# A convolution layer in a two-layer encoder trunk: order of its tiles, turning of rows, dealing of taps, and a last layer by split weights

## The chip, the core and the metric

The kernel runs on one core of a Trainium2 chip. A core has five engines that matter here, each with an instruction queue of its own that is worked off in order: TensorE (PE, matrix products; its weight loads are shown apart as PEld), VectorE (DVE), ScalarE (ACT), GpSimd (POOL), and SyncE (SP), which issues most DMAs. The metric is device time of one launch in microseconds (us), lower is better.

## The reference

Two layers in the manner of a Conformer on 256 rows of 1024 channels, all in float32. Each layer is half a SwiGLU feed-forward net (FFN, width 2816), a mixer, and half an FFN again; the first mixer is a convolution module, the second is latent attention. The change is in and around the convolution module:

```
def conv_module(h, w_pw1, w_dw, g_norm, w_pw2):
    u = h @ w_pw1
    a, b = jnp.split(u, 2, axis=-1)
    u = a * jax.nn.sigmoid(b)
    u = lax.conv_general_dilated(u, w_dw[:, None, :], ..., padding=[(30, 0)],
                                 feature_group_count=D_MODEL)
    u = jax.nn.silu(rmsnorm(u, g_norm))
    return u @ w_pw2
```

So: a norm, a product to 2048 columns, a gate, a causal depthwise convolution with 31 taps for each channel, a second norm over the channels, silu, and a last product of 1024 by 1024.

## The kernel before

**Rows and tiles.** The 256 rows are two row blocks of 128 (tb = 0, 1). A tile k or i of the convolution is 128 channels, eight in all, with channels on the partitions and rows along them.

**Weights.** `blocks` lists every weight block of 128x2048 in the order of use; `load_to` issues loads on SP into one of 3 `raw` buffers, then converts each in two pieces to a rounded high part (L160, ACT) and the remainder (L161, DVE) in `hi` and `lo`, of which there are W_BUFS = 4 each. `weights` takes the next block and loads W_BUFS - 2 = 2 ahead. Blocks marked "whole" stay float32 in `raw`. A product by split weights is three TensorE instructions (high by low, high by high, low by high: L242, L245, L246 in `mm3`); a product of plain float32 is one instruction that the trace records twice.

**Order.** The program is written as one sequence; a scheduler places instructions on the engines' queues by a simulated timeline. `urgent` marks what it is to prefer, `order(ins, first)` puts one instruction behind another, and `behind` keeps conversions behind the last urgent instructions of their engine.

**Into the convolution.** The FFN ends in `Rows.finish`: four output tiles (row block, column half) in turn, each added to h (L506); after each, `Plain.early` works on the norm of the convolution's input: squares (L269), a power on POOL (L279), and a matrix with the row factors on its diagonal (L405). `Plain.turn` multiplies h by this matrix on TensorE (L411), which scales and transposes in one plain float32 product, and copies the result with the channel gain to X on ACT and DVE (L420, L422). The second row block is turned in `late`, behind the first tile's products.

**The convolution** (`conv_in`). `products` (L636) makes gate and u of a tile, tiles 0 and 1 by row block, the rest at full width; `glu` (L643, L644) writes V. The taps of eight tiles are dealt to three engines by CONV_DVE (`taps_dve`, L678 to L681), CONV_POOL (`taps_pool`: products with the tap on ACT, L696 and L700, sums on POOL, L701 and L702) and CONV_PE (`taps_pe`, L711: products with a diagonal matrix made earlier at L1113). Tiles 6 and 7 are shared and done by row block. Squares (L723) of each tile are summed over the channels on TensorE (`total`, L729); `ends` adds the shares of tiles 6 and 7 (L802) and sums them last; `normed` makes the row factor (L746, L748, L754), spreads it over the partitions by a product with ones (L756), and writes Z = silu(Y x factor x gain) (L761, L763), for features 0 to 3 also as high and low part (L765, L766).

**Last layer.** Features 4 to 7 first, as plain float32 (L831), then 0 to 3 by split weights; 2 row blocks x 2 column halves, 512 columns each; then the addition to h (L839). The next FFN's rows are turned (L285, L299, L303) between features of the second row block.

Of the kernel before, what the change touches and what calls it, by code (L numbers as in the profile page):

```python
# [19 lines left out]
P = 128  # L20
D = 1024
S = 256
# [17 lines left out]
W_BUFS = 4  # L40
# [6 lines left out]
CONV_DVE = ((0, 0, 31), (2, 0, 31), (4, 0, 31), (5, 0, 31), (7, 0, 13))  # L47
CONV_POOL = ((1, 0, 31), (3, 0, 31), (6, 0, 19))
CONV_PE = ((6, 19, 31), (7, 13, 31))
CONV_FIRST = (0, 1)  # L50
CONV_LAST = (6, 7)

CONV_ORDER = (0, 2, 1, 4, 3, 5, 6, 7)

CONV_PLAIN = 4
# [23 lines left out]
def trunk(ctx: ExitStack, tc: tile.TileContext, x, xt, pos, invf, gains, gfin, wdw,  # L79
# [28 lines left out]
    for i in range(2):  # L108
        for w13, w2 in ((f1w13, f1w2), (f2w13, f2w2)):

            for cc_ in range(5):
                for m in range(2):
                    blocks += [w13[i, m, 2 * cc_ + a_] for a_ in range(2)]
            blocks += [w13[i, a_, 10] for a_ in range(2)]
            blocks += [w2[i, a_] for a_ in range(NF // 2)]
            if w13 is f1w13:
                if i == 0:


                    for m in (-1, -2, 0, 1, 2, 3, 4, 5, 6, 7, -3, -4):  # L120
                        w = cw2[-m - 1] if m < 0 else cw1[m]
                        blocks += [w if -2 <= m < 0 else ("whole", w)]
                        conv_block[m] = len(blocks) - 1
                else:
                    blocks += [wa[0], wa[1], wa[2][:, :1280], wa[3][:, :1280]]
                    blocks += [wuq[2], wuq[0], wukv[0], wukv[1], wuq[1]]
                    blocks += [wo[a_] for a_ in range(H // 2)]
# [13 lines left out]

    def load(src, pieces=1):
        if isinstance(src, tuple):
            raw = rawp.tile([P, HB], F32, tag="raw", name=uid("raw"))
            nc.sync.dma_start(raw, src[1])
            return raw
        n = src.shape[-1]
        raw = rawp.tile([P, HB], F32, tag="raw", name=uid("raw"))
        hi = wp.tile([P, HB], F32R, tag="hi", name=uid("hi"))
        lo = wp.tile([P, HB], F32R, tag="lo", name=uid("lo"))  # L150
        if len(loaded) < 7:

            for i in range(pieces if len(loaded) < 4 else 1):
                c = slice(i * n // pieces, (i + 1) * n // pieces) if len(loaded) < 4 else slice(n)
                fetch(raw[:, c], src[:, c])
        else:
            nc.sync.dma_start(raw[:, :n], src)
        for i in range(pieces):
            c = slice(i * n // pieces, (i + 1) * n // pieces)
            behind(nc.scalar.copy(hi[:, c], raw[:, c]))  # L160
            behind(nc.vector.tensor_sub(lo[:, c], raw[:, c], hi[:, c].bitcast(F32)))  # L161
        return hi, lo
# [36 lines left out]
    xk = const.tile([P, KT, S], F32, name="xk")  # L199
# [66 lines left out]
    def squares(ss, src, n, i, scale_in=1.0, after=()):  # L266
# [4 lines left out]
        for a in after:  # L271
            order(sq, a.ins)

# [110 lines left out]
    class Plain:  # L384

        def __init__(self, gname, act):
# [4 lines left out]
            self.dg = [xp.tile([P, P], F32, tag=f"dR{tb}", name=uid("dR")) for tb in range(NT)]  # L393

        @urgent
        def half(self, tb, i):
            squares(self.ss[tb], h[tb], D, i)
            if tb == 0 and i == 1:

# [3 lines left out]
        def diagonal(self, tb):  # L403
            r = power(self.ss[tb], D, "R")
            nc.vector.tensor_scalar(self.dg[tb], ident, r, None, op0=ALU.mult)  # L405

        @urgent
        def turn(self, tb, q, after=()):
            b = bank("B", "tp")
            for j in range(4):  # L410
                mm = nc.tensor.matmul(b[:, j * P:(j + 1) * P], h[tb][:, (4 * q + j) * P:(4 * q + j + 1) * P],  # L411
                                      self.dg[tb], start=True, stop=True)
                for a in after:
                    order(mm, a.ins)
                self.turned.append(mm)
            for j in range(4):
                k = 4 * q + j
                g = G[:, self.col + k:self.col + k + 1]
                if j % 2 == 0:
# [4 lines left out]
        def early(self, i):  # L424
            self.half(i // 2, i % 2)
            if i % 2 == 1:
                self.diagonal(i // 2)
# [113 lines left out]
    def ffn_in(act, X, make_next, beside):  # L541
        Gh = act.tile([P, NF, S], F32R, tag="Gh", name=uid("Gh"))
        Gl = act.tile([P, NF, S], F32R, tag="Gl", name=uid("Gl"))
        def turn(c, tb, w, g):
# [9 lines left out]
            b = act.tile([P, 512], F32, tag="gb", name=uid("gb"), bufs=3)  # L554
# [7 lines left out]
        for c in range(6):  # L562
# [5 lines left out]
            for m in range(1 if both else 2):  # L568
                parts = weights(KT // kn, X.whole or c > 0 or m > 0)
# [10 lines left out]
                for i, (k, tb, *kinds) in enumerate(steps):  # L580
# [9 lines left out]
                    if X.whole and c == 0 and m == 0:  # L590
                        if i == 5:
                            load_to(4)
# [10 lines left out]
            for tb in range(NT):  # L603
                s = tmp.tile([P, 512], F32, tag="s", name=uid("s"))
                nc.scalar.activation(s[:, :w], u[0, tb][:, :w], AF.Silu, scale=X.r[tb])  # L605
                g = tmp.tile([P, 512], F32, tag="g", name=uid("g"))
                nc.vector.tensor_mul(g[:, :w], s[:, :w], u[0, tb][:, w:] if both else u[1, tb])  # L607
                turn(c, tb, w, g)
# [11 lines left out]
    def conv_in(act, X, make_next):  # L620
# [10 lines left out]
        def products(i, part, t, u):  # L631

            w = loaded[conv_block[i]]
            for k in range(KT):
                c = slice(k * 2 * P + part * P, k * 2 * P + (part + 1) * P)
                mm = nc.tensor.matmul(u[:, t], w[:, c], X.x[:, k, t], start=(k == 0), stop=(k == KT - 1))  # L636
            return mm
# [9 lines left out]

        steps = [(i, tbs(tb)) for tb in range(NT) for i in CONV_FIRST]
        steps += [(i, every) for i in range(KT) if i not in CONV_FIRST]
        for n, (i, t) in enumerate(steps):  # L650
            load_to(conv_block[min(i + 2, KT - 1)] + 1)
            gate, u = bank("A", "gate"), bank("A", "u")
            products(i, 1, t, gate)
            mm = products(i, 0, t, u)
            glu(i, t, gate, u)
            if n == 0:
                X.late((mm,))

        behind(nc.scalar.activation(small.tile([P, 1], F32, tag="silu", name="silu2"), neghalf, AF.Silu))
        load_to(conv_block[-4] + 1)  # L660
        n_used[0] = max(conv_block.values()) + 1
# [7 lines left out]
        def taps_dve(k, j0, j1, t):  # L669
# [4 lines left out]
            for j in range(j0, j1):  # L674
# [4 lines left out]
                else:  # L679
                    nc.vector.scalar_tensor_tensor(out if j == j1 - 1 else y, v, w, y, op0=ALU.mult, op1=ALU.add)  # L680
            nc.vector.tensor_add(out, acc[(j1 - j0) % 2][:, c], out)  # L681

        sums_pool = []

        def taps_pool(k, j0, j1, t):
# [6 lines left out]
            for j in range(j0, j1):  # L692
# [4 lines left out]
                else:  # L697
                    p = act.tile([P, S], F32, tag="prod", name=uid("prod"), bufs=6)
                    p = p[:, :t.stop - t.start]
                    nc.scalar.activation(p, v, AF.Copy, scale=w)  # L700
                    sums_pool.append(nc.gpsimd.tensor_tensor(o, o, p, op=ALU.add))  # L701
            sums_pool.append(nc.gpsimd.tensor_tensor(y[0], y[0], y[1], op=ALU.add))  # L702
# [17 lines left out]
        def square(k, t):  # L720
            if k not in sq:
                sq[k] = act.tile([P, S], F32, tag="sq", name=uid("sq"), bufs=4)
            nc.scalar.activation(sq[k][:, t], Y[:, k, t], AF.Square)  # L723
# [8 lines left out]
        Z = act.tile([P, KT, S], F32, tag="Z", name="Z")  # L732
        Zh = act.tile([P, KT - CONV_PLAIN, S], F32R, tag="Zh", name="Zh")
        Zl = act.tile([P, KT - CONV_PLAIN, S], F32R, tag="Zl", name="Zl")

        rows_order = [*range(KT - CONV_PLAIN, KT), *range(KT - CONV_PLAIN)]
# [3 lines left out]
        zs = []  # L740

        @urgent
        def normed(tb, after=()):

            ms = small.tile([P, 1], F32, tag="msc", name=uid("msc"))
            nc.scalar.activation(ms, msb[tb][:, :1], AF.Identity, scale=1.0 / D, bias=eps)  # L746
            rc = small.tile([P, 1], F32, tag="rc", name=uid("rc"))
            power = nc.gpsimd.tensor_tensor(rc, ms, neghalf, op=ALU.pow)  # L748
            if tb == 0:

                for ins in sums_pool[-4:]:
                    order(ins, power.ins)
            dg = act.tile([P, P], F32, tag="dg", name=uid("dg"), bufs=2)
            nc.scalar.activation(dg, ident, AF.Copy, scale=rc)  # L754
# [4 lines left out]
            for k in rows_order:  # L759
                z = act.tile([P, P], F32, tag="z", name=uid("z"), bufs=6)  # L760
                zs.append(nc.vector.tensor_mul(z, Y[:, k, tbs(tb)], rb[:, :P]))  # L761
                g = G[:, g0 + k:g0 + k + 1]
                nc.scalar.activation(Z[:, k, tbs(tb)], z, AF.Silu, scale=g)  # L763
                if k < KT - CONV_PLAIN:
                    nc.scalar.activation(Zh[:, k, tbs(tb)], z, AF.Silu, scale=g)  # L765
                    nc.vector.tensor_sub(Zl[:, k, tbs(tb)], Z[:, k, tbs(tb)], Zh[:, k, tbs(tb)].bitcast(F32))  # L766
# [28 lines left out]
        def ends(tb, after, after_row):  # L795
# [4 lines left out]
            def add():  # L800
                for k in CONV_LAST:
# [4 lines left out]
                    square(k, t)  # L806
# [9 lines left out]
        ends(0, done[1][n // 2 + 1], done[1][n * 3 // 4 + 1])  # L816
        order(done[1][-3], brow[0].ins)
# [4 lines left out]
        def mm(n, tb, d):  # L822
            f = rows_order[n]
            after = ()
            if (tb, d) == (0, 0):
                after = {4: [sums[1]], 5: [brow[1]]}[n] if n in (4, 5) else ()
            w = loaded[conv_block[-1 - f // 2]]
            c = slice(f % 2 * D + d * 512, f % 2 * D + d * 512 + 512)
            start, stop = n == 0, n == KT - 1
            if f >= KT - CONV_PLAIN:  # L830
                return nc.tensor.matmul(o[tb, d], Z[:, f, tbs(tb)], w[:, c], start=start, stop=stop)  # L831
            else:
                hi, lo = w
                return mm3(o[tb, d], Zh[:, f, tbs(tb)], Zl[:, f, tbs(tb)], hi[:, c], lo[:, c], start, stop, after)

        @urgent
        def add(tb, d):
            c = slice(d * 512, d * 512 + 512)
            nc.vector.tensor_add(h[tb][:, c], o[tb, d], h[tb][:, c])  # L839

        nxt = None
        load_ahead()
        for tb in range(NT):
            for d in range(2):
                o[tb, d] = bank("A", "o")
            for f in range(KT):
                now = [mm(f, tb, d) for d in range(2)]
                if tb == 0 and f == 0:
                    first = now
                if tb == 0 and f == 2:  # L850

                    ends(1, first[1], now[1])
                if tb == 1 and f in (1, 3):
                    nxt.part(0, f // 2)
                if tb == 1 and f == 3:
# [53 lines left out]
    def rope(dst, src, n, cc, sn, tb):  # L909
# [3 lines left out]
        t2 = tmp.tile([P, 512], F32, tag="g", name=uid("rp2"))  # L913
# [14 lines left out]
    def mla_in(act, X, make_next, cc, sn):  # L928
# [36 lines left out]
        def key_rope(u, tb):  # L965
# [3 lines left out]
            for i in range(2):  # L969
                rope(kd[:, i, :], kx.rearrange("p (n i f) -> p n i f", n=1, i=2), 1, cc, sn, tb)  # L970
# [38 lines left out]
        for tb in range(NT):  # L1009
# [8 lines left out]
            rope(q, u.rearrange("p (n i f) -> p n i f", i=2, f=32), H, cc, sn, tb)  # L1018
# [206 lines left out]
```

## Time and profile before

| | us |
|---|---|
| median of three runs (lowest to highest) | 934.76 (934.67 to 935.11) |
| the profiled execution | 934.88 |
| its span, first to last instruction | 932.8 |
| first gate product of the convolution (L636) | 187.6 |
| last start of a tap on TensorE (L711) | 261.8 |
| last layer of the convolution on TensorE | 262.2 to 289.7 |
| DVE waits for POOL's part (L802 behind L702), in all | 1.7 |
| POOL waits for the first product (L701 behind L700) | 8.0 |
| POOL waits for a product at 242.4 | 1.8 |

All times of the form "at 262.2" are us from the span's start. "128*128 128x512" is a product of a 128x128 weight with 512 columns. The durations of TensorE's instructions overlap, so what one costs is the time from its start to the next one's.

### The profile page before, as it was taken

To read this page: it belongs to the slowest core of one execution; us is meant where nothing else is said; L and a number is where in the kernel's file an instruction comes from. 1 tells how busy PE (TensorE), PEld (TensorE's weight loads), DVE (VectorE), ACT (ScalarE), POOL (GpSimd) and SP (SyncE) were. 2 spreads that over 40 slices of the span, in tenths; PEclk is the share of its full clock that TensorE was granted. 3 is DMA by queue.
4 is the path that set the end of the run, shared out by engine and by line. 5 is a ranking of instruction groups with operands and counts; after the bars stand their busy time and mean duration, and the time that the engine had idled before them with its cause. 6 is when DMAs were issued, how large, how long until landed. Compare 5 with 4: busy or idle time off the path is not lost.

```text
span 932.8 us, 12069 instructions
## 1 busy us (share of the span) xinstructions
PE 924.0 (99%) x4394; PEld 771.8 (83%) x4394; DVE 577.0 (62%) x907; ACT 496.0 (53%) x849; POOL 85.2 (9%) x210
## 2 busy tenths in 40 slices
PE   9999999999999999999999999999999999999997
PEld 7888888898967888888888888888898888888886
DVE  5776664489965655655466666644666676656643
ACT  7964443468866444434465445434676574445431
POOL 1000000059920000000000000000200000000000
PEclk9999999999999999999999999999999999999999
DMA  9886775524315876766537677754451467767721
GB/s 338 301 313 234 249 253 193 180 92 141 131 52 209 281 229 225 265 208 231 208 142 274 226 240 251 253 187 142 172 189 46 182 231 246 244 226 254 242 91 45
DMA packets 60826, 191.54 MB, mean 205 GB/s; under 512 B 11232, under 2 KB 33376, under 8 KB 41440
## 3 DMA queue, kind: packets, MB, share of 16 engines
q1 hardware_dynamic: 60192, 190.09, 58.5%
q8 instruction: 34, 0.56, 0.2%
q10 hardware_dynamic: 576, 0.69, 0.2%
q14 instruction: 24, 0.20, 0.1%
HBM read 178.17 MB, written 12.58 MB: 205 GB/s over the span
## 4 chain that ended last, share of the span: by engine, by line
PE 94%; DVE 2%; ACT 2%; DMA 1%; issue 0%; POOL 0%; POOLq 0%; ACTq 0%; DVEq 0%
PE u L242 17%; PE u L245 17%; PE u L246 17%; PE o L245 10%; PE o L242 10%; PE o L246 10%; PE gate L636 3%; PE u L636 3%; PE y L711 1%; DVE lo L161 1%; PE u L251 1%; PE tp L285 1%; PE o L831 1%; DMA raw<-in_f2w 1%; PE sc L1049 0%
## 5 line engine op out<-in xcount | busy, mean ns | idle before, releaser
L161 DVE TENSOR_TENSOR lo<-raw,hi 128x1024 fp32r<-128x1024 f32 (+1 forms) x290 | 339.5, 1212 | 200.3 <-ACT hi L160 200.0
L160 ACT CAST hi<-raw 128x1024 fp32r<-128x1024 f32 (+1 forms) x290 | 288.8, 1049 | 267.1 <-PE u L246 128.1
L242 PE MATMUL u<-lo,Xh 128*128 128x512 f32 x688 | 268.1, 390 | 0.0
L245 PE MATMUL u<-hi,Xh 128*128 128x512 f32 x688 | 267.8, 389 | 0.0
L246 PE MATMUL u<-hi,Xl 128*128 128x512 f32 x688 | 267.7, 390 | 0.0
L242 PEld LDWEIGHTS u<-lo,Xh 128*128 128x128 f32 x688 | 129.2, 188 | 27.2 <-DVE lo L161 0.4
L246 PEld LDWEIGHTS u<-hi,Xl 128*128 128x128 f32 x688 | 129.2, 188 | 26.8
L245 PEld LDWEIGHTS u<-hi,Xh 128*128 128x128 f32 x688 | 129.2, 188 | 26.7
L245 PE MATMUL o<-hi,Gh 128*128 128x512 f32 (+1 forms) x356 | 137.9, 387 | 0.0
L246 PE MATMUL o<-hi,Gl 128*128 128x512 f32 (+1 forms) x356 | 137.7, 387 | 0.0
L242 PE MATMUL o<-lo,Gh 128*128 128x512 f32 (+1 forms) x356 | 137.4, 388 | 0.0
L242 PEld LDWEIGHTS o<-lo,Gh 128*128 128x128 f32 x356 | 66.9, 188 | 13.6
L246 PEld LDWEIGHTS o<-hi,Gl 128*128 128x128 f32 x356 | 66.9, 188 | 13.5
L245 PEld LDWEIGHTS o<-hi,Gh 128*128 128x128 f32 x356 | 66.9, 188 | 13.3
L276 POOL TENSOR_TENSOR ms<-ss 128x1 f32<-128x1 f32 x16 | 4.6, 287 | 635.3 <-ACT junk L269 635.3
L560 DVE TENSOR_TENSOR Gl<-gb,Gh 128x512 fp32r<-128x512 f32 (+1 forms) x48 | 30.9, 644 | 43.6 <-ACT Gh L559 43.6
L559 ACT CAST Gh<-gb 128x512 fp32r<-128x512 f32 (+1 forms) x48 | 28.0, 584 | 53.9 <-DMA gb<-gd 53.7
L680 DVE SCALAR_TENSOR_TENSOR acc<-V,dw,acc 128x256 f32<-128x256 f32 (+1 forms) x160 | 53.9, 416 | 0.0
L700 ACT ACTIVATE prod<-V,dw 128x128 f32<-128x128 f32 (+1 forms) x121 | 46.1, 420 | 3.0 <-POOL odd L701 1.3
L607 DVE TENSOR_TENSOR g<-s,u 128x512 f32<-128x512 f32 (+1 forms) x48 | 30.7, 639 | 12.4 <-PE u L246 12.4
L605 ACT ACTIVATE s<-u,R 128x512 f32<-128x512 f32 (+1 forms) x48 | 31.2, 650 | 6.7 <-ACT Gh L559 3.2
L549 DVE STREAM_TRANSPOSE gt<-g 128x512 f32<-128x512 f32 (+1 forms) x48 | 32.0, 667 | 1.6
(207 smaller groups left out, 838.0 us busy)
## 6 DMA issues: line engine op xcount, KB each, us to landing
raw<-in_f2w SPq DMA_DIRECT2D x66, 1024.0 KB, 4.9
raw<-in_f1w SPq DMA_DIRECT2D x62, 1024.0 KB, 5.0
raw<-in_cw SPq DMA_DIRECT2D x12, 1024.0 KB, 4.7
gd<-gt SPq DMA_DIRECT2D x160, 64.0 KB, 3.2
gb<-gd SPq DMA_DIRECT2D x40, 256.0 KB, 4.5
raw<-in_wo SPq DMA_DIRECT2D x4, 1024.0 KB, 5.0
raw<-in_wuq SPq DMA_DIRECT2D x3, 1024.0 KB, 4.9
raw<-in_f1w SPq DMA_DIRECT2D x8, 256.0 KB, 5.1
```

The lines of the kernel that those rows point to most:

```text
L160: behind(nc.scalar.copy(hi[:, c], raw[:, c]))
L161: behind(nc.vector.tensor_sub(lo[:, c], raw[:, c], hi[:, c].bitcast(F32)))
L242: mm = nc.tensor.matmul(o, ah, bl, start=start, stop=False)
L245: nc.tensor.matmul(o, ah, bh, start=False, stop=False)
L246: return nc.tensor.matmul(o, al, bh, start=False, stop=stop)
L549: nc.vector.transpose(t[:, :w], g[:, :w].rearrange("p (t j q) -> p j t q", t=n, q=32))
L560: nc.vector.tensor_sub(Gl[:, f, tbs(tb)].rearrange("p t (i q) -> p t i q", q=32), bv, gh.bitcast(F32))
L605: nc.scalar.activation(s[:, :w], u[0, tb][:, :w], AF.Silu, scale=X.r[tb])
L607: nc.vector.tensor_mul(g[:, :w], s[:, :w], u[0, tb][:, w:] if both else u[1, tb])
L636: mm = nc.tensor.matmul(u[:, t], w[:, c], X.x[:, k, t], start=(k == 0), stop=(k == KT - 1))
L680: nc.vector.scalar_tensor_tensor(out if j == j1 - 1 else y, v, w, y, op0=ALU.mult, op1=ALU.add)
L700: nc.scalar.activation(p, v, AF.Copy, scale=w)
```

## The change

It touches seven things.

1. W_BUFS is 5 instead of 4, so weights are loaded and converted three blocks ahead; to find room, the input xk takes a buffer of the weights, the gated product g is written over s, `gb` has two buffers instead of three, and the rope's second buffer moves to the attention's pool. In the first chunk of the first FFN the loads ahead are placed by hand.
2. `Plain` scales the rows into a tile hn, half on ACT and half on DVE, and turns them by TensorE's transpose (`transposed`) instead of the product with a diagonal; the second block's copies are all on ACT. The last square is ordered behind the conversion of the third last-layer block.
3. The products of the tiles are in one strict order, (0, tb 0), (1, tb 0), (0, tb 1), (1, tb 1), 2, 4, 3, 5, 6, 7, and the second row block is turned between gate and u of the second tile instead of behind the first.
4. Taps: tile 7 has 17 on DVE (13 before) and 14 on TensorE (18), tile 6 has 20 on POOL (19) and 11 on TensorE (12).
5. The whole last layer goes by split weights in the order 0 to 7; blocks -3 and -4 are converted too. Z is kept as high and low part alone; the gain goes into the product with the factor, and six of the eight features are done in pairs.
6. Fixed places: on DVE, POOL, ACT and TensorE the taps, sums, squares and factors of the two row blocks are ordered against each other (`order` with an index from the end of a list).
7. The first conversion of the next FFN is ordered behind the second block's Z, and its turned rows come behind features 2 and 4.

```diff
-W_BUFS = 4
+W_BUFS = 5
...
-CONV_DVE = ((0, 0, 31), (2, 0, 31), (4, 0, 31), (5, 0, 31), (7, 0, 13))
-CONV_POOL = ((1, 0, 31), (3, 0, 31), (6, 0, 19))
-CONV_PE = ((6, 19, 31), (7, 13, 31))
+CONV_DVE = ((0, 0, 31), (2, 0, 31), (4, 0, 31), (5, 0, 31), (7, 0, 17))
+CONV_POOL = ((1, 0, 31), (3, 0, 31), (6, 0, 20))
+CONV_PE = ((6, 20, 31), (7, 17, 31))
 CONV_FIRST = (0, 1)
-CONV_LAST = (6, 7)
-CONV_ORDER = (0, 2, 1, 4, 3, 5, 6, 7)
-CONV_PLAIN = 4
+CONV_STEPS = ((0, 0), (1, 0), (0, 1), (1, 1), (2, None), (4, None), (3, None), (5, None), (6, None), (7, None))
+CONV_TILES = (0, 1, 2, 4, 3, 5, 6, 7)
+CONV_LAST = (7, 6)
+CONV_ORDER = (0, 2, 1, 4, 5, 3, 7, 6)
...
-                    for m in (-1, -2, 0, 1, 2, 3, 4, 5, 6, 7, -3, -4):
-                        w = cw2[-m - 1] if m < 0 else cw1[m]
-                        blocks += [w if -2 <= m < 0 else ("whole", w)]
+                    for m in (-1, -2, -3, *CONV_TILES, -4):
+                        blocks += [cw2[-m - 1] if m < 0 else ("whole", cw1[m])]
...
-    xk = const.tile([P, KT, S], F32, name="xk")
+    xk = wp.tile([P, HB], F32, tag="hi", name="xk").rearrange("p (k t) -> p k t", t=S)
...
-        def diagonal(self, tb):
+        def scale(self, tb):
             r = power(self.ss[tb], D, "R")
-            nc.vector.tensor_scalar(self.dg[tb], ident, r, None, op0=ALU.mult)
+            if tb == 0:
+                for hi, lo in (casts[conv_block[-3], i] for i in range(PIECES)):
+                    order(self.sq, hi.ins)
+            nc.scalar.activation(self.hn[:, tb, 512:], h[tb][:, 512:], AF.Copy, scale=r)
+            nc.vector.tensor_scalar(self.hn[:, tb, :512], h[tb][:, :512], r, None, op0=ALU.mult)
...
-            b = bank("B", "tp")
-            for j in range(4):
-                mm = nc.tensor.matmul(b[:, j * P:(j + 1) * P], h[tb][:, (4 * q + j) * P:(4 * q + j + 1) * P],
-                                      self.dg[tb], start=True, stop=True)
...
+            b = transposed(self.hn[:, tb, :], 4 * q, 4, after, self.turned)
...
-                if j % 2 == 0:
+                if j % 2 == 0 or tb == 1:
...
-            b = act.tile([P, 512], F32, tag="gb", name=uid("gb"), bufs=3)
+            b = act.tile([P, 512], F32, tag="gb", name=uid("gb"), bufs=2)
...
-                parts = weights(KT // kn, X.whole or c > 0 or m > 0)
+                parts = weights(KT // kn, c > 0 or m > 0)
+                if X.whole and c == 0 and m == 0:
+                    load_to(4)
...
-                g = tmp.tile([P, 512], F32, tag="g", name=uid("g"))
-                nc.vector.tensor_mul(g[:, :w], s[:, :w], u[0, tb][:, w:] if both else u[1, tb])
-                turn(c, tb, w, g)
+                nc.vector.tensor_mul(s[:, :w], s[:, :w], u[0, tb][:, w:] if both else u[1, tb])
+                turn(c, tb, w, s)
...
+        mm = None
+        for n, (i, tb) in enumerate(CONV_STEPS):
...
-            products(i, 1, t, gate)
-            mm = products(i, 0, t, u)
+            mm = products(i, 1, t, gate, mm)
+            if n == 1:
+                X.late((mm,))
+                mm = X.turned[-1]
+            mm = products(i, 0, t, u, mm)
             glu(i, t, gate, u)
-            if n == 0:
-                X.late((mm,))
...
+            dgs.append(nc.scalar.activation(dg, ident, AF.Copy, scale=rc))
             if tb == 0:
-                for ins in sums_pool[-4:]:
+                for ins in pool_last[-16:]:
                     order(ins, power.ins)
+                order(prods_last[-6], ms_ins.ins)
+                order(prods_last[-4], dgs[0].ins)
...
-            for k in rows_order:
-                z = act.tile([P, P], F32, tag="z", name=uid("z"), bufs=6)
-                zs.append(nc.vector.tensor_mul(z, Y[:, k, tbs(tb)], rb[:, :P]))
-                g = G[:, g0 + k:g0 + k + 1]
-                nc.scalar.activation(Z[:, k, tbs(tb)], z, AF.Silu, scale=g)
-                if k < KT - CONV_PLAIN:
-                    nc.scalar.activation(Zh[:, k, tbs(tb)], z, AF.Silu, scale=g)
-                    nc.vector.tensor_sub(Zl[:, k, tbs(tb)], Z[:, k, tbs(tb)], Zh[:, k, tbs(tb)].bitcast(F32))
+            for k in (range(0, 1), range(1, 2), range(2, 4), range(4, 6), range(6, 8)):
+                z = act.tile([P, 2, 2, P], F32, tag="z", name=uid("z"), bufs=3)
+                n = len(k)
+                for j in k:
+                    zs.append(nc.vector.scalar_tensor_tensor(z[:, 0, j - k[0], :], Y[:, j, tbs(tb)],
+                                                             G[:, g0 + j:g0 + j + 1], rb[:, :P],
+                                                             op0=ALU.mult, op1=ALU.mult))
+                k = slice(k[0], k[0] + n)
+                zhs.append(nc.scalar.activation(Zh[:, k, tbs(tb)], z[:, 0, :n, :], AF.Silu))
+                nc.scalar.activation(z[:, 1, :n, :], z[:, 0, :n, :], AF.Silu)
+                zls.append(nc.vector.tensor_sub(Zl[:, k, tbs(tb)], z[:, 1, :n, :],
+                                                Zh[:, k, tbs(tb)].bitcast(F32)))
+            if tb == 0:
+                for ins in dve_last[-5:]:
+                    order(ins, zs[1].ins)
+                for ins in prods_last[-7:]:
+                    order(ins, zhs[1].ins)
...
+                    if tb == 0:
+                        for ins in dve_last[3 - CONV_DVE[-1][2]:][:2]:
+                            order(ins, last.ins)
+                        order(prods_last[-10], sq_ins.ins)
...
-        ends(0, done[1][n // 2 + 1], done[1][n * 3 // 4 + 1])
-        order(done[1][-3], brow[0].ins)
+        ends(0, done[1][11], done[1][20])
+        order(done[1][12], sums[0].ins)
+        order(done[1][21], brow[0].ins)
...
+                for kinds in ("lh", "x") if f < 2 else ("lhx",):
+                    now = [mm(f, tb, d, kinds) for d in range(2)]
+                if tb == 0 and f == 4:
+                    then = now[1]
...
+                elif tb == 0 and f == 6:
+                    ends(1, then, now[0])
+                    for p in behind_sums:
+                        order(p, sums[1].ins)
+                    later[0, 7, 0] = later[0, 7, 1] = [brow[1]]
+                    for i in range(PIECES):
+                        hi, lo = casts[max(conv_block.values()) + 1, i]
+                        order(hi, zhs[7].ins)
+                        order(lo, zs[-1].ins)
+                if tb == 1 and f in (2, 4):
+                    nxt.part(0, f // 2 - 1, (now[1],))
...
```

Here `done[1]` lists the second row block's taps on TensorE (25 after the change), `pool_last`, `prods_last` and `dve_last` the sums on POOL, the products on ACT and the accumulating taps on DVE in order of writing, `zs`, `zhs` and `zls` the scaled rows and the high and low parts.

## Prediction

> **What bounds the kernel now.** I read the page first, then the chain that ended last, then windows through the convolution, then TensorE's own instructions in order of time there.
>
> ```profile
> PE 924.0 (99%) x4394; PEld 771.8 (83%) x4394; DVE 577.0 (62%) x907; ACT 496.0 (53%) x849; POOL 85.2 (9%) x210
> PE 94%; DVE 2%; ACT 2%; DMA 1%; issue 0%; POOL 0%; POOLq 0%; ACTq 0%; DVEq 0%
> ```
>
> The reader sees TensorE (PE) busy 924.0 of 932.8 us, and 94% of the chain on it. A saved TensorE instruction is therefore worth its spacing to the next one, as long as nothing else takes the place. Windows of the convolution (columns: window, length, busy time and count of PE, PEld, DVE, ACT, POOL, clock, DMA share, GB/s):
>
> ```profile
> 198.50:221.00 22.50, 22.50 (x129) 20.44 (x129) 22.18 (x74) 21.38 (x65) 22.46 (x55) 1.00 0.49 173
> 221.00:242.00 21.00, 21.00 (x99) 18.51 (x98) 20.62 (x54) 16.77 (x41) 20.92 (x34) 1.00 0.44 157
> 245.00:256.50 11.50, 11.50 (x104) 11.47 (x103) 9.74 (x31) 10.27 (x28) 10.96 (x26) 1.00 0.27 93
> ```
>
> While the taps run, VectorE (DVE) and GpSimd (POOL) are as full as TensorE: a gain on TensorE alone ends where it must wait for their sums. TensorE's timeline (start, duration, line, tiles, count; the start-to-start time is the price):
>
> ```profile
> 261.22 0.83 PE L711 MATMUL y<-V,diag 128*128 128x128 f32 x6
> 262.20 7.13 PE L831 MATMUL o<-raw,Z 128*128 128x512 f32 x16
> 268.77 0.79 PE L242 MATMUL o<-lo,Zh 128*128 128x512 f32 x1
> 269.40 0.39 PE L245 MATMUL o<-hi,Zh 128*128 128x512 f32 x1
> ...
> 276.19 7.14 PE L831 MATMUL o<-raw,Z 128*128 128x512 f32 x16 [0.65 <-ACT Z L763]
> 283.17 1.04 PE L285 MATMUL tp<-ident,h 128*128 128x128 f32 x8
> ```
>
> A plain float32 product of 512 columns is two records: 16 records from 276.19 to 283.17 are 8 products, 0.873 us each. A split product is three records at 0.229 (from 284.51 on), 0.687. Waits: 6 tap records at 0.112 from 261.22 end at 261.89, the next starts at 262.20 (0.31); 268.77 lasts 0.79 where its kind lasts 0.39 (0.40); the split products end their pace at 275.37, next start 276.19 (0.82). Together 1.53 us.
>
> **The change part by part, on TensorE.** *Turning rows* (L411 to a transpose of rows scaled beforehand): the chain has 16 records of L411 as 1.79 us per row block, and 8 transposes of L285 as 0.87. Saved 2 x 0.92 = 1.84. A page of the Trainium skill speaks against this (TensorE: Matmul & The Clock Gate, Part 4: PE-mode transpose): transposes do not count as activity for the clock and take some 275 ns each in a kernel. Eight of L285 do last 0.27 each here but start 0.109 apart, and the window around them has clock 1.00; the trace disagrees, and by the rule the sum would be 2.6 us worse.
>
> *Taps*: tiles 6 and 7 have 12+18 taps on TensorE, then 11+14; 5 fewer in each row block, 10 products of two records, 46 records in 5.24 us (0.114): 10 x 0.228 = 2.28 saved. *Last layer*: of 4 plain features x 2 row blocks x 2 column halves, 16 products become split: 16 x (0.873 - 0.687) = 2.98 saved. Sum 7.1 us, and 1.5 of waits that can also go: 8.6 at most.
>
> **What the other engines pay.** Times below are on the old trace's clock. The first row block's turning saves 0.92, so the gates start at 186.7 instead of 187.62; its scaling needs both halves of 512 columns (0.6 to 0.75 by L605 and L506, instead of 0.29 for L405), 0.4 us more, under the TensorE products that fill 184.4 to 186.7. The strict order makes u of tile 1 end at 186.7 + 4 x 1.79 + 0.87 = 194.7 instead of 196.7; GpSimd, which waited 8.0 us for its first product, starts at 196.5 instead of 198.54. On ScalarE (ACT) the second block's eight copies (0.3 each, four more than before) stand in 192.5 to 195.2, just ahead of that.
>
> GpSimd: 60 adds of 128 columns at 0.414 apart (starts 198.54, 198.95, ...) for tile 1 end at 221.4. Tile 3, now behind tile 4, gets its V at 186.7 + 14.3 (eight half-tile products of 1.79) + 0.9 (turning) + 3 x 6.9 (a wide tile is 2 x 3.45 in the chain) + 0.7 (drain and L644) = 223.3 and its first product 1.4 later (two copies and a product of L696/L700 on ACT): 224.7, an idle stretch of 3.3 us that the old order did not have. 30 adds at 0.687 to 245.3, 19 adds of tile 6 (one more tap) to 253.2. VectorE: starts 1.7 earlier, loses four copies of L422 (1.0), gains one row scaling (0.4) and four taps at 0.257 (1.0) in the first row block: its sum for tile 7, ready after 254.75 and held until 256.48 by the GpSimd part, comes at 253.9. TensorE: with 1.84 and 2.28 less its taps would end at 257.8; the total is pinned ahead of the last 13 taps, at 254.5. Both adds and squares (0.3 + 0.3 each, as L802 and L723) put the total at 254.5 to 255.5. I take 0.7 us of wait. From a total's start to the row's sum took 1.8 (259.20 to 260.99), to the last layer's first product 1.2 more: 258.5, against TensorE's free time 257.8 + 0.7; no second wait over 0.3.
>
> The second row block: GpSimd has 16 adds behind the power at 255.8, whose last 7 products wait on ACT for the second high Z; ends near 262.7; the total is pinned behind feature 4 of the first block, 258.6 + 5 x 1.37 (six records of 0.229) = 265.5, so 2 us are in hand. The fourth weight block's conversion (2 x 1.05 ACT, 2 x 1.22 DVE, new here) has from 261 to feature 6 at 266.8. FFN2's first conversion, which together with its load held the Z ahead of 276.19, is pinned behind them. New waits in all: 1.2 us taken, from 0 to 6 (bounds: all hidden; or GpSimd with the old gaps of 1.76 and 0.47 us, three adds of the other block ahead at 0.41, and a conversion of 2.0 in front).
>
> **Costed at nothing, and its cover.** Five weight buffers and three blocks ahead: conversions move one block (5.4 us) earlier; the third layer block is converted at 175.1, where the second was, before the square at 181.3 that is made to follow it. Loads of conv tiles keep their times, since the raw buffer each needs is freed by the same event. If that cover were gone, a late conversion costs 2.0 + 2.4 us. Two gb buffers for three: the last low part (L560) of a chunk ends at 126.7, the next gb load goes out on SP at 129.9, 3.2 us in hand; else SP's weight loads behind it shift by the rest. g within s: its transpose ends 10 us or more before the next use. xk in a weight buffer: read until 12 us, the block that follows in it is the fifth. Gain from deeper buffers: none, as TensorE's weight loads waited 0.4 us for a conversion in the whole run.
>
> **Sum.** 934.88 (the profiled execution, span 932.8 and 2.1 around it) - 7.1 - 1.5 + 1.2 = 927.5. The median of the runs shown, 934.76, is 0.1 lower; I keep 927.5.
>
> **Rivals.**
> All hidden: no new wait, 934.88 - 8.6 = 926.3. For it: VectorE and TensorE meet within 0.2 us in my count. Against: GpSimd's new idle stretch. 0.14.
> GpSimd sets the hand-over: the old gaps stay and three adds go first, its part of the first block at 256.6, total at 257.2 against 254.5: 2.7 instead of 0.7, so 929.5, and 931.5 with one conversion ahead of the Z. For it: POOL is busy 20.92 of 21.00. Against: six adds of the second block ran ahead of that part before, at most three may now. 0.17.
> Slower: conversions, issued a block earlier, stand in ACT's queue ahead of the attention layer's exponentials (L1064). Each pair is 2.0 us; five blocks are loaded between 690 and 745: 10 us, 937.5. It decides once over 7.3 us of this is uncovered. For it: at 703.74 a pair does stand between two exponentials. Against: TensorE has 0.3 us or less of each wait there, with other heads and the output layer to run. 0.12, and 0.04 that about half of it cancels the gain.
> Transposes that take their whole duration: 16 x 0.27 = 4.3 instead of 1.75, 930.1 (the mechanism of the skill's page above). 0.02.
>
> **Chances.** Forecast 0.51, its own range 926.6 to 928.9. The predicted time is its. With the first two rivals 0.82 lie within 925.9 to 931.6, the range. A measurement tells 0.2% (1.9 us) from no change. Faster 0.51 + 0.14 + 0.17 + 0.02 = 0.84; same 0.04; slower 0.12.
>
> **What would show it.** L285 with 16 more transposes and no L411; 100 tap records instead of 120; the last layer without L831, all in threes; TensorE reaching the first of these near 258.7 and FFN2 near 282.5 (289.72 before). The wait for GpSimd's or VectorE's part shows at the total (L729) between taps. I am wrong if a wait of over 3 us stands there, or if windows behind 290 keep a different length than before.

## The result, and the profile after

| | us |
|---|---|
| before, median of 8 runs | 934.77 |
| changed, median of 8 runs (lowest to highest) | 932.0 (930.86 to 932.71) |
| ratio, changed to before (95% interval) | 0.9969 (0.9958 to 0.998) |
| the profiled execution of the changed kernel, and its span | 930.86, 929.1 |
| first gate product of the convolution | 186.51 (187.62 before) |
| first product of the last layer on TensorE | 261.24 (262.20) |
| first product of the next FFN | 284.91 (289.56) |

The change gains 2.8 us in the median where 7.3 were forecast, and the time lies above the range. The page of the changed kernel shows the removed work: 20 TensorE instructions fewer, and 5 us less of TensorE busy time.

```profile
PE 918.9 (99%) x4374; PEld 772.2 (83%) x4374; DVE 584.7 (63%) x917; ACT 499.7 (54%) x852; POOL 90.0 (10%) x212
PE 94%; DVE 2%; ACT 1%; POOL 1%; issue 1%; DMA 0%; POOLq 0%; ACTq 0%; DVEq 0%
```

What went wrong stands in one place. TensorE's timeline there (start, duration, line, tiles, count; in brackets the idle time before it and its releaser):

```profile
253.30 0.91 PE L716 MATMUL y<-V,diag 128*128 128x128 f32 x6
255.08 0.38 PE L734 MATMUL ms<-ones,sq 128*128 128x1 f32 x2 [0.86 <-ACT sq L728]
256.24 0.38 PE L734 MATMUL ms<-ones,sq 128*128 128x1 f32 x2 [0.77 <-ACT sq L728]
256.48 2.97 PE L716 MATMUL y<-V,diag 128*128 128x128 f32 x18
259.24 0.63 PE L761 MATMUL rb<-dg,ones 128*128 128x128 f32 x2
259.67 1.81 PE L716 MATMUL y<-V,diag 128*128 128x128 f32 x8
261.24 0.48 PE L849 MATMUL o<-lo,Zh 128*128 128x512 f32 x1
```

TensorE stops twice: for the square of tile 7 (total at 255.08) and for that of tile 6 (256.24). Beyond the pace of the instructions before them these waits are 1.03 and 0.91, together 1.94 us. Then 18 tap records take 2.97 us from first start to last end; at full clock the same 18 take 2.25 (the half-filled kernel below). The second view, one-us windows of TensorE alone (window, length, busy time and count, granted clock, DMA share, GB/s), says why:

```profile
256.00:257.00 1.00, 0.77 (x6) 1.00 0.00 0
257.00:258.00 1.00, 1.00 (x11) 0.91 0.00 0
258.00:259.00 1.00, 1.00 (x6) 0.50 0.00 0
259.00:260.00 1.00, 1.00 (x7) 0.50 0.00 0
260.00:261.00 1.00, 1.00 (x7) 0.50 0.00 0
261.00:262.00 1.00, 1.00 (x6) 0.88 0.00 0
```

The granted clock, 1.00 until then, is 0.50 from 257.82 to 261.23: 3.41 us. From the first tap of tile 6 behind the totals (256.48) to the last layer takes 4.76 us. In the kernel with the order 2, 3, 4 below, which keeps the clock, the same instructions take 3.26:

```profile
255.70 2.25 PE L716 MATMUL y<-V,diag 128*128 128x128 f32 x18
258.96 0.50 PE L849 MATMUL o<-lo,Zh 128*128 128x512 f32 x1
```

So the clock costs 1.50 us on top of the pause. The Trainium skill (TensorE: Matmul & The Clock Gate, Part 1) gives the clock a free-running window of 3413 ns, and that length agrees. Its rule to avoid idle gaps over some 3.4 us (HAM oscillation, in that part) would have let this pause pass; here two pieces of idle of 0.86 and 0.77 us were enough, and the measurement decides.

Why the square of tile 6 was late shows in GpSimd's timeline of the changed kernel:

```profile
224.52 0.73 POOL L706 TENSOR_TENSOR Y<-Y,prod 128x256 f32<-128x256 f32 x1 [3.40 <-ACT prod L705]
...
253.94 0.98 POOL L706 TENSOR_TENSOR odd<-odd,prod 128x128 f32<-128x128 f32 x2
255.00 0.45 POOL L707 TENSOR_TENSOR part<-part,odd 128x128 f32<-128x128 f32 x1
```

Tile 3 starts at 224.52 behind an idle stretch of 3.40 (forecast 224.7 and 3.3), but the part of tile 6 is done at 255.45, not 253.2: three adds of the second row block, 0.414 each, went in between, and an idle gap of 0.52 at 242.4. These make up 1.76 of the 2.25 us; where the rest went wasn't told apart. VectorE adds this part as soon as it is there:

```profile
255.49 0.29 DVE L818 TENSOR_TENSOR Y<-y,part 128x128 f32<-128x128 f32 x1 [0.77 <-POOL part L707]
```

The square of tile 7 waited for another reason. VectorE's sum was there at 253.92, as forecast (253.9), but ScalarE squared it only at 254.73, behind a run of tap products (start, duration, count):

```profile
251.94 2.88 ACT L705 ACTIVATE prod<-V,dw 128x128 f32<-128x128 f32 x7
254.73 0.29 ACT L728 ACTIVATE sq<-Y 128x128 f32<-128x128 f32 x1
255.87 0.31 ACT L728 ACTIVATE sq<-Y 128x128 f32<-128x128 f32 x1 [0.85 <-DVE Y L818]
```

This second delay sets where the pause is divided, not how long it is: the total of tile 6 stands behind that of tile 7, and its square waited for GpSimd's part alone.

Two smaller losses lie behind the convolution. TensorE's start of the next FFN, in the changed kernel:

```profile
286.29 0.60 PE L290 MATMUL tp<-ident,h 128*128 128x128 f32 x4
287.35 0.50 PE L246 MATMUL u<-lo,Xh 128*128 128x512 f32 x1 [0.46 <-ACT Xh L304]
287.69 0.40 PE L249 MATMUL u<-hi,Xh 128*128 128x512 f32 x1
```

The product of the second row block at 287.35 needs the copy of rows that were turned only at 286.29; it stalls TensorE while products of the first row block stand behind it. This costs 0.6: from the first product of that FFN to the end of the span it takes 644.14 us in the kernel with 18 taps on GpSimd below, and 643.56 in the one that also orders these products otherwise. The last line to see is in the list of waits by group (all, count, longest):

```profile
PE ms L734 <- ACT sq L728: 1.6, 2, 0.9
...
PE u L246 <- ACT Xh L304: 0.5, 1, 0.5
PE nope L246 <- DVE rp L959: 0.4, 1, 0.4
```

The third is in the attention layer, at 682.3, and takes 0.32 more than its like before (0.66 from the start of the instruction ahead of it, where it was 0.34).

### The profile page after: what moved, and what is told of

Its sections match the earlier page's. It is cut to its first block, busy times and chain, and to the rows that moved or that the text cites. A ratio compares the mean times of both kernels' runs of the same rounds, so it can differ in the third digit from the quotient of the medians.

```text
span 929.1 us, 12053 instructions
## 1 busy us (share of the span) xinstructions
PE 918.9 (99%) x4374; PEld 772.2 (83%) x4374; DVE 584.7 (63%) x917; ACT 499.7 (54%) x852; POOL 90.0 (10%) x212
## 4 chain that ended last, share of the span: by engine, by line
PE 94%; DVE 2%; ACT 1%; POOL 1%; issue 1%; DMA 0%; POOLq 0%; ACTq 0%; DVEq 0%
PE u L246 17%; PE u L249 17%; PE u L250 17%; PE o L246 9%; PE o L249 9%; PE o L250 9%; PE gate L640 3%; PE u L640 3%; PE o L849 2%; PE tp L290 1%; PE u L255 1%; DVE lo L163 1%; PE y L716 0%; PE sc L1089 0%; PE a L250 0%
## 5 line engine op out<-in xcount | busy, mean ns | idle before, releaser
L163 DVE TENSOR_TENSOR lo<-raw,hi 128x1024 fp32r<-128x1024 f32 x294 | 344.2, 1212 | 191.0 <-ACT hi L162 190.7
L162 ACT CAST hi<-raw 128x1024 fp32r<-128x1024 f32 x294 | 292.7, 1048 | 254.7 <-PE o L250 87.7
L281 POOL TENSOR_TENSOR ms<-ss 128x1 f32<-128x1 f32 x16 | 8.0, 502 | 630.8 <-ACT junk L273 630.8
L684 DVE SCALAR_TENSOR_TENSOR acc<-V,dw,acc 128x128 f32<-128x128 f32 (+1 forms) x168 | 56.0, 415 | 0.0
L611 DVE TENSOR_TENSOR s<-s,u 128x512 f32<-128x512 f32 (+1 forms) x48 | 30.5, 636 | 10.6 <-PE u L250 10.5
L553 DVE STREAM_TRANSPOSE gt<-s 128x512 f32<-128x512 f32 (+1 forms) x48 | 32.0, 667 | 1.4
```

Source lines behind the costliest of these rows:

```text
L162: casts[len(loaded), i] = (nc.scalar.copy(hi[:, c], raw[:, c]), nc.vector.tensor_sub(lo[:, c], raw[:, c], hi[:, c].bitcast(F32)))
L553: nc.vector.transpose(t[:, :w], g[:, :w].rearrange("p (t j q) -> p j t q", t=n, q=32))
L611: nc.vector.tensor_mul(s[:, :w], s[:, :w], u[0, tb][:, w:] if both else u[1, tb])
L684: dve_last.append(nc.vector.scalar_tensor_tensor(out if j == j1 - 1 else y, v, w, y, op0=ALU.mult, op1=ALU.add))
```

## The experiments

The theory: the pause at the totals costs twice, once by its own length and once by the clock that falls behind it; the rest of the change does what it says. The rivals: the 18 records are slow for another reason (weights, memory, the other engines), and the deal of the taps is the fault, or the work removed elsewhere was worth less than counted. Before was measured beside each group of runs, at 934.89 to 934.91.

**Fill the pause.** Products of a tile of zeros, 256 columns each, keep TensorE busy while it waits: nine ahead of tile 7's total, eight ahead of tile 6's. They are written to columns that nobody reads; for that, the buffer of the row's sum is taken earlier.

```diff
+FILL = {7: 9, 6: 8}
...
+                        for _ in range(FILL[k]):
+                            mm = nc.tensor.matmul(early_rb[:, 256:], still[:, :P], still, start=True, stop=True)
```

> Seventeen small products with zeros stand on TensorE where it waited for the two totals of the first row block (9 ahead of tile 7's, 8 ahead of tile 6's; 0.107 us each at full clock, 1.8 us in all against waits of 1.03 and 0.91). Nothing else of the work changes. Theory A (the pause is paid twice: once as itself, and once as a TensorE clock granted at 0.50 for 3.4 us or a multiple behind it): the granted clock stays at 1.00 through the convolution, the first product of the last layer starts near 259.6 instead of 261.2, and the time is 929.0 to 929.5 with a spread under 0.5 us. Theory B (the clock's fall is not brought about by the pause, or costs nothing): the same as the changed kernel, 930.9 to 932.7.

Measured: 930.28 us (4 runs), ratio 0.995 (0.9936 to 0.9965). The clock stays at 1.00 through the convolution, and from the first gate to the last layer it takes 73.25 us instead of 74.73. That the clock is the cost is right; the expected time was missed by 0.8. In this trace 0.33 of it is a later start of the gates (186.84), which isn't the work of the fill: the changed kernel itself has 186.86 in its second profile. The other 0.47 is a longer last layer (23.91 from its first product's start to its last one's, instead of 23.44). Of this, 0.42 lies at the first low part of Z, at 261.42: TensorE came earlier, and what it met next was late.

**Both once more, on one chip.** The changed kernel and the filled one, five runs each.

> The changed kernel itself, on one chip with the kernel whose pause is filled. Theory A (the fall of the clock is brought about by the pause): the clock falls to 0.50 for 3.4 or 6.8 us in every run, 931 to 933. Theory B (it was that chip's): no fall, 930.2 to 930.6.

> The pause filled with 17 small products, beside the changed kernel on one chip. Theory A: no fall of the clock, 1.4 to 2.5 us under the changed kernel with its pause at the same length. Theory B: the same time as the changed kernel within 0.5 us.

Measured: 931.85 and 930.43, ratios 0.9967 (0.9954 to 0.9979) and 0.9952 (0.9938 to 0.9965): 1.42 us between them. Windows of all engines (length, busy time and count of PE, PEld, DVE, ACT, POOL, granted clock, DMA share, GB/s) of the changed kernel, and then of the filled one:

```profile
255.00:259.00 4.00, 2.79 (x18) 2.71 (x19) 2.69 (x11) 2.27 (x8) 2.38 (x6) 0.84 0.01 2
259.00:263.00 4.00, 4.00 (x22) 3.60 (x22) 2.30 (x10) 2.09 (x9) 2.79 (x7) 0.73 0.00 0
```

```profile
255.00:259.00 4.00, 4.00 (x37) 3.60 (x35) 2.62 (x10) 2.27 (x8) 2.38 (x7) 1.00 0.01 2
259.00:263.00 4.00, 3.88 (x21) 3.00 (x21) 3.76 (x14) 3.44 (x14) 4.00 (x11) 1.00 0.00 0
```

In 255 to 259 the other engines do nearly the same in both (VectorE 2.69 and 2.62, ACT 2.27 in 8 instructions, GpSimd 2.38), and the DMA share is 0.01. What differs is TensorE's own idleness, and with it the clock. So the rival that weights, memory or other engines slow the 18 records falls.

**Fill half of it.** The eight products ahead of tile 6's total alone, `FILL = {7: 0, 6: 8}`: a single gap is left.

> The changed kernel with only the second half of the pause filled (8 small products ahead of tile 6's total), so a wait of about 1.0 us stays ahead of tile 7's. Theory A (the clock falls only if a pause is long enough for a stretch of fixed length to look idle, and where that stretch begins changes from run to run): the clock falls in none or some of the runs; 930.2 to 931.0, with a larger spread than with both halves filled where it does. Theory B (any pause of this place brings it down): all runs near 931.5 to 932.5.

Measured: 930.16 (930.0 to 930.39, 4 runs), ratio 0.9949 (0.9935 to 0.9964), no fall of the clock in any run (mean 0.998 or more in each). TensorE's timeline of this kernel:

```profile
255.66 0.38 PE L735 MATMUL ms<-ones,sq 128*128 128x1 f32 x2 [0.85 <-ACT sq L729]
255.91 1.03 PE L835 MATMUL rb<-still 128*128 128x256 bf16 x8
257.07 2.25 PE L717 MATMUL y<-V,diag 128*128 128x128 f32 x18
```

One idle gap of 0.85 leaves the clock alone, and the 18 records take 2.25 instead of 2.97. A second gap of nearly the same size just behind it, in the changed kernel, brings it down. Where between the two the bound lies wasn't tried.

**Wide tiles in the order 2, 3, 4** (CONV_STEPS, and CONV_TILES to match). This undoes the late tile 3 of GpSimd: its 3.4 us idle stretch came of putting tile 4 first.

```diff
-... (2, None), (4, None), (3, None), (5, None), ...
+... (2, None), (3, None), (4, None), (5, None), ...
```

> The wide tiles in the order 2, 3, 4 again (as before the change), so GpSimd gets tile 3 one tile (6.9 us) earlier. Theory A (the total waits for GpSimd's part, which is late because GpSimd idles 3.4 us for tile 3): the idle stretch at 221 goes, GpSimd's part of the first block comes near 252 instead of 255.4; VectorE waits some 0.8 us for tile 4 and its sum for tile 7 comes near 254.9, so the pause at the total shrinks from 1.9 to about 1.0 us and the clock stays at 1.00: 928.3 to 929.0. Theory B (VectorE, not GpSimd, sets the total): the pause stays at 1.9 us or grows to 2.7, 931.5 to 933.

Measured: 929.95 (929.46 to 930.73, 4 runs), ratio 0.9947 (0.9932 to 0.9962). GpSimd runs through (its first adds of tile 3, the wide ones, at 220.06 and 221.58), its part of tile 6 is done at 252.25, and only one wait is left:

```profile
PE ms L734 <- ACT sq L728: 0.7, 1, 0.7
```

That wait is now VectorE's: its sum of tile 7 starts at 254.53, 0.61 later than in the changed kernel. The last layer starts at 258.96. From the first gate to there it takes 72.18 us, 2.55 less than in the changed kernel; some 2.4 were expected (0.9 of pause, 1.5 of clock). The time was missed all the same, by 0.95 in the median and 0.46 in the profiled run: in this trace the gates start 0.27 later, the last layer is 0.47 longer, and from the next FFN on it takes 0.31 longer. Two of the four runs are 1 us longer, at a mean clock of 0.996 and 0.997 instead of 0.998; they have no trace, so that the clock falls in these is argued, not shown.

**Fewer taps on GpSimd, more on TensorE.** Tile 6 with 18 taps on GpSimd and 13 on TensorE, which puts 0.91 us of work back (4 products by 0.228).

```diff
-CONV_POOL = (..., (6, 0, 20))
-CONV_PE = ((6, 20, 31), (7, 17, 31))
+CONV_POOL = (..., (6, 0, 18))
+CONV_PE = ((6, 18, 31), (7, 17, 31))
```

> Tile 6 gives two of GpSimd's taps to TensorE (18 and 13 instead of 20 and 11). GpSimd's part comes 0.83 us earlier, TensorE has 4 products of 0.228 = 0.9 us more to do. Theory A: the pause falls to 0.6 to 0.9 us, the clock stays at 1.00, 928.8 to 929.4. Theory B (the pause alone counts): 930.5 to 931.5.

Measured: 929.07 (928.63 to 929.54, 4 runs), ratio 0.9938 (0.9922 to 0.9955), as expected, though the trace shows no idle gap at the totals where a pause of 0.6 to 0.9 us was expected. The clock doesn't fall, and the last layer starts at 258.82. More work on the engine that bounds the kernel made it 2.9 us faster than the changed kernel in the median; in the traces 2.57 of it lie between the first gate and the last layer.

**Taps dealt as before**, the rest of the change kept: 13 on VectorE, 19 on GpSimd, 12 and 18 on TensorE.

> The changed kernel with the taps dealt as before the change (13 of tile 7 on VectorE, 19 of tile 6 on GpSimd, 18 and 12 on TensorE). TensorE has 10 products, 2.3 us, more. Theory A: the pause is 0.7 us or less, the clock stays at 1.00, and the time is 929.5 to 930.3, less than with the new dealing although TensorE does more. Theory B: 932 to 933, the new dealing's 10 products missing.

Measured: 931.29 (931.25 to 931.38, 4 runs), ratio 0.996 (0.9946 to 0.9975); the clock does not fall. From gate to last layer takes 73.42 us, 0.17 more than with the new deal and the pause filled: of the 2.28 us of taps taken off TensorE, nearly all came back as waiting. The expected time was missed by about 1.0: the gates start 0.5 later, and the span ends 7.85 after the last product's start instead of 6.60. About 1.0 of that lies behind ScalarE's last computing instruction, which ends at 925.14 here and at 925.63 in the changed kernel; only the output still has to be written then. Why this takes longer stays open.

**The turning alone**, in the kernel before.

> The kernel before with rows scaled first and turned by TensorE's transpose, nothing else. Theory A (a transpose costs its spacing of 0.109 us, the product with the diagonal 0.224): 1.84 us less on TensorE, but the second block's 0.92 stands where VectorE and GpSimd set the end of the taps as well, so 933.0 to 934.0. Theory B (transposes cost their whole 0.27 us, or slow the clock): 935.5 or more.

Measured: 933.76 (10 runs), ratio 0.9988 (0.9978 to 0.9997). The gates start at 186.64 instead of 187.62. Two views of this kernel, TensorE's timeline and its waits:

```profile
184.39 1.04 PE L285 MATMUL tp<-ident,hn 128*128 128x128 f32 x8
```

```profile
PE rb L751 <- ACT dg L749: 0.6, 1, 0.6
```

The eight transposes take 1.04 from first start to last end, as long as the eight at 283.17 in the kernel before. Of the 1.84 us saved, 1.1 reach the end in the median. In this trace the first row block's 0.98 is there at the gates; the second's is lost by the last layer (74.57 us from gate to last layer, 74.58 before), most of it in a new wait for the row factor. That the wait stands there because GpSimd and VectorE had not become faster is inferred.

**The buffers alone**, in the kernel before: five weight buffers and what makes room for them.

> The kernel before with part 1 of the change alone: five weight buffers and three blocks ahead, xk in one of them, two gb buffers, g over s, the rope's buffer moved. Theory A (it costs and brings nothing): 934.6 to 935.2. Theory B (the 1.3 us that the changed kernel loses behind 290 us come from the deeper conversions): 935.6 to 936.4.

Measured: 935.23 (934.88 to 936.03, 10 runs), ratio 1.0004 (0.9995 to 1.0013): no difference that can be told. But its list of waits has the line in the attention layer that the changed kernel has too:

```profile
PE nope L242 <- DVE rp L919: 0.4, 1, 0.4
```

That instruction starts 0.67 behind the one ahead of it here and 0.34 in the kernel before. The turning alone has no such line, so the 0.33 us lost there come from this part.

**A better version.** 18 taps on GpSimd as above, and in the next FFN the second row block's first products ordered behind those of the first.

```diff
+                        if X.between is not None and c == 0 and m == 0 and (k, tb) == (0, 1):
+                            after = [tb0_last]
-                        mm3(u[m, tb], *args, k == 0, k == KT - 1, after)
+                        tb0_last = mm3(u[m, tb], *args, k == 0, k == KT - 1, after)
```

> The kernel with 18 taps of tile 6 on GpSimd, and in the next FFN's first chunk the second row block's products ordered behind the first block's. Theory A (the new wait of 0.6 us at the start of that FFN comes from two products of the second row block that stand on TensorE's queue right behind the first turned part, before its copies can be there): the wait goes, 928.3 to 928.7. Theory B (the turned rows come late because conversions stand ahead of the copies on ScalarE): the wait only moves to the second block, 929.0 to 929.3.

Measured: 928.06 (927.97 to 928.25, 4 runs), ratio 0.9926 (0.991 to 0.9943): the fastest kernel here, 1.0 below the one without the second edit in the median, which was taken in another group of runs; 0.58 of it stand in the traces behind the start of the next FFN, where the edit works. Its timeline at the totals:

```profile
253.77 1.36 PE L718 MATMUL y<-V,diag 128*128 128x128 f32 x10
255.06 0.64 PE L736 MATMUL ms<-ones,sq 128*128 128x1 f32 x4
255.57 2.25 PE L718 MATMUL y<-V,diag 128*128 128x128 f32 x18
259.14 0.48 PE L851 MATMUL o<-lo,Zh 128*128 128x512 f32 x1
```

Taps, totals and taps follow without an idle gap; from the first gate (186.98) to the last layer it is 72.16 us, where the prediction counted 72.0. That the two agree is partly luck: this kernel does 0.91 us more on TensorE than the one predicted, and has no pause where the prediction took 0.7.

**Order 2, 3, 4 with the taps dealt out again:** 15 on VectorE, 21 on GpSimd, 10 and 16 on TensorE, and the strict FFN.

> Tile 3 ahead of tile 4 again, 15 taps of tile 7 on VectorE, 21 of tile 6 on GpSimd, 16 and 10 on TensorE (26, one more than in the changed kernel, one fewer than with 18 on GpSimd), and the next FFN's second block behind its first. Theory A (GpSimd, given its tile early, carries three taps more than with 18, and TensorE's two products of 0.228 fewer come through): 927.4 to 927.9, with a pause under 0.4 us at the totals. Theory B (VectorE, waiting 0.8 us for tile 4, sets the totals): a pause of 0.5 to 0.9 us, 928.1 to 928.7.

Measured: 928.28 (928.0 to 928.42, 5 runs), ratio 0.9928 (0.9916 to 0.9941). Neither theory holds: there is no pause, as the first said, but the time is in the range of the second. From the first gate to the last layer it takes 71.76 us, 0.40 less than in the kernel above; the last layer (23.81) is 0.25 longer, and from the next FFN on it takes 0.37 longer. So what the deal gains in the convolution is lost behind it.

## Why the prediction was wrong, point by point

- **Work removed from TensorE (7.1): right.** 100 tap records, 16 transposes for two row blocks, a last layer all in threes. From its first product's start to its last one's, the last layer takes 23.44 us instead of 27.12: 2.98 of work, and 0.7 of the waits it had. The gates start at 186.51, forecast 186.7. (The 289.72 that the prediction gives for FFN2 before is the end of the last layer; its first product starts at 289.56.)
- **Three times of the other engines: right within 0.2 us**, tile 3's start, the idle stretch ahead of it, and VectorE's sum.
- **The step that failed** is "I take 0.7 us of wait" at the total, in "New waits in all: 1.2 us taken". Two things were wrong in it. First, its size: the pause is 1.94 us. GpSimd's part came at 255.45 and not at "253.2": the three adds of the other row block that the pin allows (1.24 us) and the gap of 0.52 were put into the upper bound and not into the estimate, and 0.5 more is not told apart. The order 2, 3, 4, which brings GpSimd's part to 252.25, leaves a single wait of 0.7. The square of tile 7 behind tap products on ScalarE wasn't counted either, but it only divided the pause. Second, its price: a wait was priced at its own length. Behind this one the clock halves for 3.41 us, which costs 1.5 more. The filled kernel shows the two apart: same lateness of the sums, no fall, 1.42 us less. Together the first product of the last layer came at 261.24 instead of 258.7.
- **Costed at nothing.** Two waits behind the last layer had no term: the scheduler put two products of the second row block where their rows were not yet copied (0.6), and the deeper buffers cost 0.3 in the attention layer. The better version removes the first. The 3 us bound named for a wait at the total was not reached; the other sign named, windows behind 290 of another length, did come: from the first product of the next FFN to the end it takes 644.19 us instead of 643.24.
- **The sum again:** 927.5, less 0.2 (earlier gates) plus 1.25 (pause) plus 1.5 (clock) plus 0.6 and 0.3 make 931.0; the profiled execution has 930.86. The median is 1.1 above it. The four longest of its eight runs have a mean clock of 0.995 to 0.996 where the profiled one has 0.997, and 0.1 to 0.2% of 930 is 0.9 to 1.9 us. That the clock stays low longer in them is likely, but they have no trace.
- **Rivals.** "GpSimd sets the hand-over" named the mechanism, three adds ahead of its part, and came nearest; it too left out the clock. The conversions in front of the attention's exponentials did nothing of the size feared: the buffers alone are 1.0004 of before. Transposes at their whole duration did not occur: eight take 1.04 us in the changed kernel (at 184.25) as before. The prediction's "the trace disagrees" holds for their spacing of 0.109 us. Whether transposes count as activity for the clock isn't shown by eight of them, which are over in 1.04 us between other products.

## What to carry to other kernels

When work is taken off the engine that bounds a kernel, first write down when each of the other engines delivers, with every instruction that may stand ahead on their queues, and deal out only as much as they cover: here 4 products put back on TensorE were worth 2.9 us. Two short pauses on TensorE close together can cost more than their length, so look at the granted clock in one-us windows behind them. Where the pause stayed here, products of zeros into unused columns kept the clock.

## What the runs showed of the hardware

Two idle gaps of 0.86 and 0.77 us (254.22 to 256.24, with one small product between them) were followed by a granted clock of 0.50 for 3.41 us. The second profile of the changed kernel shows the same, with gaps of 0.86 and 0.78. The clock fell only after TensorE had work again: 1.58 us after the second gap in the first profile (at 257.82), 1.12 in the second (at 257.71). One gap of 0.85 us (half filled) or 0.72 (order 2, 3, 4) was not followed by a fall, in their profiles. Whether the small product between the gaps counts as work, and what sum or share of idle time is the bound, isn't shown. Products of zeros do count as work for the clock: with 17 of them in the gaps it stayed at 1.00. Eight float32 transposes from 184.39 on, 1.04 us in all, left it at 1.00 as well.
